# A decoder layer's opening in source order: x in smaller pieces between one-tile weight batches, squares later, idle transposes first

## The chip, the cores and the metric

One core of one Trainium2 chip runs the kernel; the other cores are not used. The metric is the device time of one execution in microseconds, the median of several runs. A difference under 0.2% (some 3.7 us here) can't be told from no change.

## The reference

One layer, batch 1, 256 positions of width 2048, all in fp32. It is a feed-forward half-step, an attention mixture of three head groups, and a second feed-forward half-step:

```python
def swiglu(x, w_gate, w_up, w_down):
    return (jax.nn.silu(x @ w_gate) * (x @ w_up)) @ w_down

x = x + 0.5 * swiglu(rms_norm(x, ffn1_norm[l]), ffn1_gate[l], ffn1_up[l], ffn1_down[l])
h = rms_norm(x, mix_norm[l])
...
x = x + mixed @ w_out[l]
x = x + 0.5 * swiglu(rms_norm(x, ffn2_norm[l]), ffn2_gate[l], ffn2_up[l], ffn2_down[l])
```

The inner width of the feed-forward is 5632. The change concerns only the start of the first gate product, x @ ffn1_gate.

## The kernel before

**Products.** Each fp32 product is made of three fp32r matmuls. A weight is cast to fp32r (`hi`, ACT) and the rest of it is kept as a second fp32r tile (`lo` = raw − hi, DVE). `mm_rows` does, for each of the two 128-row halves of x, hi·wh, hi·wl and lo·wh (L248 to L250), so one 128-row tile of a 512-wide weight block takes six matmuls of 512 columns. Weights come in batches of two such tiles: `load_w` (L198) issues one 512 KB DMA on SP's queue (tile `raw`, four buffers), the ACT cast (L205, three buffers of `hi`) and the DVE subtract (L206, three of `lo`). In the names, `ag` is gate of the first feed-forward, `au` its up weights, and the number is the first tile: `raw_ag_6` holds tiles 6 and 7. `ga` and `ua` are their PSUM accumulators. Gate and up take 16 tiles for each of eleven 512-wide column blocks, always gate, then up.

**x.** The stationary side is x0T, x transposed and scaled by the norm's gain, also as hi and lo. `transpose_chunk` (L213) makes it from 128x128 transposes on PE into a PSUM tile (`tp_x_4` holds tiles 4 to 7; tags `l0` and `l1`, one buffer each), an ACT copy with scale for hi (L226) and a DVE scalar_tensor_tensor for lo, which reads the same PSUM tile and the hi just written (L227). The chunks before are tiles 0-1, 2-3, 4-7, 8-11 and 12-15 (`XCUT`, L109). x is loaded in the same pieces, the first on SP's queue, the others on ACT's.

**Norm.** The row scale (1/rms) is only needed after the first gate block, so the squares of x (`square_sums`, L233 to L236, ACT, eight of 512 columns) run beside the matmuls; `row_rstd` and `rsqrt` then make the scale on DVE.

**Order.** Generators in a class `Lanes` are stepped by `tick` once for each weight batch, and `finish` forces one to its end; `before0` finishes a chunk ahead of the batch that needs it. Beyond the order in which the code emits, the framework's scheduler chooses, for each engine, the order of the instructions by its own priorities. The instructions of an engine then run strictly in that order. `constants` (L139) loads small parameters on POOL's queue, makes masks there, and later transposes the gains (L172, tile `gps`, tag `l0`), copies them to `gT` (L174) and negates the sinks (`nsink`, L178, DVE).

Of the kernel before, what the change touches and what calls it, by code (L numbers as in the profile page):

```python
# [11 lines left out]
AF = mybir.ActivationFunctionType  # L12
ALU = mybir.AluOpType
# [65 lines left out]
def hybrid_layer(ctx, tc, x, mem, ffn1_norm, ffn1_gate, ffn1_up, ffn1_down, mix_norm, mem_norm,  # L79
# [18 lines left out]
    def psum(tag, name):  # L98

        return ps.tile([P, 2, 512], F32, tag=tag, bufs=2 if tag == "acc" else 1, name=name)  # L100

    lanes = Lanes()


    x_sb = cpool.tile([P, NT, D], F32, name="x_sb")
    xv = x.rearrange("(t p) d -> p t d", p=P)
    graw1 = cpool.tile([NK, P], F32, name="graw1")
    nc.scalar.dma_start(graw1, ffn1_norm[0].rearrange("(k p) -> k p", p=P))
    XCUT = ((0, 2), (2, 2), (4, 4), (8, 4), (12, 4))  # L109
    for k0, nk in XCUT:  # L110
        cols = slice(k0 * P, (k0 + nk) * P)
        (nc.scalar if k0 else nc.sync).dma_start(x_sb[:, :, cols], xv[:, :, cols])

    ident = cpool.tile([P, P], F32, name="ident")
    make_identity(nc, ident)
# [2 lines left out]
    warm = cpool.tile([P, 1], F32, name="warm")  # L118
    nc.scalar.activation(warm, ones[:, 0:1], AF.Silu)

    gT = cpool.tile([P, 4 * NK + 6], F32, name="gT")
    gps = psum("l0", "gps1")
    nc.tensor.transpose(gps[:, 0, 0:NK], graw1, ident[0:NK, 0:NK])
    nc.vector.tensor_copy(gT[:, 0:NK], gps[:, 0, 0:NK])
    G_FFN1, G_MIX, G_MEM, G_FFN2, G_HEAD = 0, 16, 32, 48, 64
# [72 lines left out]
    def load_w(w, k0, nk, c0, width, name):  # L198
        raw = wpool.tile([P, KB, 512], F32, tag="raw", bufs=4, name=f"raw_{name}")
        hi = wpool.tile([P, KB, 512], F32R, tag="hi", bufs=3, name=f"hi_{name}")  # L200
        lo = wpool.tile([P, KB, 512], F32R, tag="lo", bufs=3, name=f"lo_{name}")
        r, h, l = (t[:, :nk, :width] for t in (raw, hi, lo))
        nc.sync.dma_start(
            r, w[k0 * P:(k0 + nk) * P, c0:c0 + width].rearrange("(k p) c -> p k c", p=P))
        nc.scalar.copy(h, r)  # L205
        nc.vector.tensor_tensor(out=l, in0=r, in1=h.bitcast(F32), op=ALU.subtract)  # L206
        return h, l
# [2 lines left out]
        nc.scalar.copy(dst_hi, src)  # L210
        nc.vector.tensor_tensor(out=dst_lo, in0=src, in1=dst_hi.bitcast(F32), op=ALU.subtract)

    def transpose_chunk(xT, src, k0, nk, g0, name, pause=1):  # L213

        def stages(tag):
            sv, dst = src(), xT()
            tp = psum(tag, f"tp_{name}")
            tv = tp.rearrange("p a b -> p (a b)").rearrange("p (k s) -> p k s", k=4)
            for k in range(nk):
                for t in range(NT):  # L220
                    nc.tensor.transpose(tv[:, k, t * P:(t + 1) * P], sv[:, t, k * P:(k + 1) * P], ident)
            if pause:
                yield pause
            for k in range(nk):
                g = gT[:, g0 + k0 + k:g0 + k0 + k + 1]
                nc.scalar.activation(dst[:, k0 + k, 0, :], tv[:, k, :], AF.Copy, scale=g)  # L226
                nc.vector.scalar_tensor_tensor(out=dst[:, k0 + k, 1, :], in0=tv[:, k, :], scalar=g,  # L227
                                               in1=dst[:, k0 + k, 0, :].bitcast(F32), op0=ALU.mult,
                                               op1=ALU.subtract)
            yield 1  # L230
        return stages
# [11 lines left out]
    def mm_rows(acc, aT, kt, wh, wl, first, last):  # L243

        w = wh.shape[-1]
        for t in range(NT):
            hi, lo = aT[:, kt, 0, t * P:(t + 1) * P], aT[:, kt, 1, t * P:(t + 1) * P]
            nc.tensor.matmul(acc[:, t, :w], hi, wh, start=first, stop=False)  # L248
            nc.tensor.matmul(acc[:, t, :w], hi, wl, start=False, stop=False)  # L249
            nc.tensor.matmul(acc[:, t, :w], lo, wh, start=False, stop=last)  # L250

    def project(acc, aT, w, c0, width, kts, nk_all, done, name, before=None):

        for k0, n in kts:
            k = k0
            while k < k0 + n:
                b = min(KB, k0 + n - k)
                if before:
                    before(k)
                wh, wl = load_w(w, k, b, c0, width, f"{name}_{k}")  # L260
                for j in range(b):
                    mm_rows(acc, aT, k + j, wh[:, j, :], wl[:, j, :], done == 0, done == nk_all - 1)
                    done += 1
                k += b
                lanes.tick()
        return done


    def ffn(xT, before, stats, wg, wu, wd, after, name):

        with tc.tile_pool(name=f"h_{name}", bufs=1, reuse_waits="tile") as hpool, \
                tc.tile_pool(name=f"ht_{name}", bufs=2, reuse_waits="tile") as htmp:
            hT = hpool.tile([P, NF, 2, SEQ], F32R, name=f"hT_{name}")

            def transpose_h(j, h):

                def stages(tag):
                    tp = psum(tag, f"th_{name}{j}")
# [12 lines left out]
            rstd = None
            for j in range(DFF // 512):
                acc = psum("acc", f"g{name}{j}")
                project(acc, xT, wg, j * 512, 512, [(0, NK)], NK, 0, f"{name}g{j}",
                        None if j else before)
                if j == 0:
                    rstd = stats()
                g = htmp.tile([P, NT, 512], F32, tag="g", bufs=3, name=f"gs{name}{j}")
                for t in range(NT):
                    nc.scalar.activation(g[:, t, :], acc[:, t, :], AF.Silu, scale=rstd[:, t:t + 1])  # L300
                acc = psum("acc", f"u{name}{j}")
                project(acc, xT, wu, j * 512, 512, [(0, NK)], NK, 0, f"{name}u{j}")
                for t in range(NT):
                    nc.vector.scalar_tensor_tensor(out=g[:, t, :], in0=acc[:, t, :],
                                                   scalar=rstd[:, t:t + 1], in1=g[:, t, :],
                                                   op0=ALU.mult, op1=ALU.mult)
                lanes.put(f"hT{name}{j}", transpose_h(j, g))

            def before_d(k):
                if k >= NF - 4:  # L310
                    lanes.finish(f"hT{name}{DFF // 512 - 1}")

            for c in range(4):
                acc = psum("acc", f"d{name}{c}")
# [14 lines left out]
    ss2 = cpool.tile([P, NT, 4], F32, name="ss2")  # L329
    x0T = r1.tile([P, NK, 2, SEQ], F32R, tag="r1", name="x0T")  # L330

    for k0, nk in XCUT:
        cut = x_sb[:, :, k0 * P:(k0 + nk) * P]
        lanes.put(f"aT{k0}", transpose_chunk(lambda: x0T, lambda cut=cut: cut, k0, nk, G_FFN1, f"x0_{k0}", 0))

    def before0(k):
        if k in (0, 2, 4, 8, 12):
            lanes.finish(f"aT{k}")

    def sum_stages(ss, src, c, wait=None):  # L340
        yield 2 + c if wait is None else wait
        square_sums(ss, src(c), c)

    for c in range(4):
        lanes.run(f"ss0_{c}", sum_stages(ss0, xchunk, c))
    lanes.put("consts", constants, ("aT12",))

    memv = mem.rearrange("(t p) d -> p t d", p=P)
    memTs = []
# [22 lines left out]
        square_sums(ss1, xchunk(c), c)  # L372

    def stats0():
        lanes.finish(*(f"ss0_{c}" for c in range(4)))
        return row_rstd(ss0, "x0")

    ffn(x0T, before0, stats0, gate1, up1, down1, after1, "a")
    memT = memTs[0]
    lanes.finish("memT3")  # L380

# [310 lines left out]
        lanes.finish("ss2_3")  # L692
        return row_rstd(ss2, "x2")

    ffn(x2T, lambda k: lanes.finish("bT3") if k == 12 else None, stats2, gate2, up2, down2, store, "b")


# [29 lines left out]
```

## Time and profile before

| | |
|---|---|
| runs of the kernel before | 1846.38 us median of 3 (1846.11 to 1847.82) |
| the profiled execution | 1845.47 us, of which its span is 1843.7 us |
| PE busy | 1829.9 us, 99% of the span |
| PE's share of the chain that ended last | 97% |
| ACT busy, DVE busy | 846.4 us (46%), 938.9 us (51%) |
| HBM read | 339.83 MB, 185 GB/s over the span |

The span is what the hardware profiler recorded of one execution on the core. The first gate matmul starts at 10.23 us of it and the first up matmul at 36.14 us; the change lies in that stretch and the microseconds before it.

### The profile page before, as it was taken

The page shows a single profiled execution, that of the slowest core. Times are in us where ns is not written, and L with a number is a line of the kernel's source. Part 1 is how long each engine was busy: PE and PEld are TensorE (multiplying, and loading weights), DVE is VectorE, ACT ScalarE, POOL GpSimd, SP SyncE. Part 2 cuts the span into 40 slices and gives each one's busy share as a digit, 9 for nine tenths or more (in the row PEclk, how much of TensorE's full clock was granted, in tenths as well). Part 3 has the DMA queues.
Part 4 walks back from the last instruction along what each step waited for, and adds up shares of the span by engine and source line. Part 5 has one row for each costly group of instructions (what it writes and reads, how often), then busy time and mean ns, then how long its engine had stood idle before and what let it go on. Part 6 is the DMA issues. An engine that isn't in the chain of part 4 may idle for free.

```text
span 1843.7 us, 21918 instructions
## 1 busy us (share of the span) xinstructions
PE 1829.9 (99%) x8448; PEld 1538.8 (83%) x8448; DVE 938.9 (51%) x1121; ACT 846.4 (46%) x1148; POOL 11.1 (1%) x31
## 2 busy tenths in 40 slices
PE   8999999999999999999999999999999999999998
PEld 6888888888888888888998888888888888888887
DVE  5554544555445554645655455555555454544443
ACT  6444444444435443656665455444444444433332
POOL 2000000000000000000000000000000000000000
PEclk9999999999999999999999999999999999999999
DMA  7666666666656566565555556666666666666663
GB/s 231 192 189 189 193 186 191 191 188 192 187 191 206 194 210 193 176 175 147 161 143 145 179 181 189 192 186 192 188 190 193 184 192 187 192 194 204 206 204 128
DMA packets 182520, 343.36 MB, mean 186 GB/s; under 512 B 11088, under 2 KB 28048, under 8 KB 182416
## 3 DMA queue, kind: packets, MB, share of 16 engines
q1 hardware_dynamic: 180368, 339.04, 61.6%
q10 hardware_dynamic: 1696, 2.89, 0.4%
q8 instruction: 66, 1.08, 0.3%
q14 instruction: 38, 0.31, 0.1%
q0 software_dynamic: 352, 0.03, 0.0%
HBM read 339.83 MB, written 2.10 MB: 185 GB/s over the span
## 4 chain that ended last, share of the span: by engine, by line
PE 97%; DMA 1%; ACT 1%; DVE 1%; issue 0%; DVEq 0%; ACTq 0%
PE ga L248 4%; PE ga L250 4%; PE ga L249 4%; PE ua L248 4%; PE gb L248 4%; PE db L249 4%; PE db L250 4%; PE gb L249 4%; PE gb L250 4%; PE ub L248 4%; PE ua L249 4%; PE ua L250 4%; PE ub L249 4%; PE ub L250 4%; PE db L248 4%; PE da L249 4%
## 5 line engine op out<-in xcount | busy, mean ns | idle before, releaser
L206 DVE TENSOR_TENSOR lo_bu<-raw_bu,hi_bu 128x1024 fp32r<-128x1024 f32 x88 | 107.8, 1225 | 131.5 <-ACT hi_bu L205 131.5
L206 DVE TENSOR_TENSOR lo_au<-raw_au,hi_au 128x1024 fp32r<-128x1024 f32 x88 | 107.8, 1225 | 130.1 <-ACT hi_au L205 130.1
L206 DVE TENSOR_TENSOR lo_bd<-raw_bd,hi_bd 128x1024 fp32r<-128x1024 f32 x88 | 107.7, 1224 | 124.0 <-ACT hi_bd L205 124.0
L206 DVE TENSOR_TENSOR lo_ad<-raw_ad,hi_ad 128x1024 fp32r<-128x1024 f32 x88 | 107.8, 1224 | 119.5 <-ACT hi_ad L205 119.5
L205 ACT CAST hi_bd<-raw_bd 128x1024 fp32r<-128x1024 f32 x88 | 92.8, 1055 | 145.0 <-PE db L250 139.8
L206 DVE TENSOR_TENSOR lo_ag<-raw_ag,hi_ag 128x1024 fp32r<-128x1024 f32 x88 | 108.1, 1229 | 98.7 <-ACT hi_ag L205 98.7
L206 DVE TENSOR_TENSOR lo_bg<-raw_bg,hi_bg 128x1024 fp32r<-128x1024 f32 x88 | 107.7, 1223 | 99.2 <-ACT hi_bg L205 99.2
L205 ACT CAST hi_ad<-raw_ad 128x1024 fp32r<-128x1024 f32 x88 | 92.7, 1053 | 131.5 <-PE da L250 106.4
L205 ACT CAST hi_bg<-raw_bg 128x1024 fp32r<-128x1024 f32 x88 | 92.7, 1054 | 127.2 <-PE gb L250 68.3
L205 ACT CAST hi_ag<-raw_ag 128x1024 fp32r<-128x1024 f32 x88 | 92.7, 1054 | 122.5 <-PE ga L250 66.3
L205 ACT CAST hi_bu<-raw_bu 128x1024 fp32r<-128x1024 f32 x88 | 92.7, 1054 | 115.5 <-PE ub L250 79.0
L205 ACT CAST hi_au<-raw_au 128x1024 fp32r<-128x1024 f32 x88 | 92.7, 1054 | 115.3 <-PE ua L250 79.4
L248 PE MATMUL ga<-hi_ag,x0T 128*128 128x512 f32 x352 | 138.7, 394 | 0.0
L248 PE MATMUL gb<-hi_bg,x2T 128*128 128x512 f32 x352 | 137.9, 392 | 0.0
L250 PE MATMUL ga<-hi_ag,x0T 128*128 128x512 f32 x352 | 137.3, 390 | 0.0
L249 PE MATMUL ga<-lo_ag,x0T 128*128 128x512 f32 x352 | 137.3, 390 | 0.0
L248 PE MATMUL da<-hi_ad,hT_a 128*128 128x512 f32 x352 | 137.2, 390 | 0.0
L249 PE MATMUL da<-lo_ad,hT_a 128*128 128x512 f32 x352 | 137.1, 389 | 0.1
L250 PE MATMUL gb<-hi_bg,x2T 128*128 128x512 f32 x352 | 137.1, 389 | 0.0
L248 PE MATMUL ua<-hi_au,x0T 128*128 128x512 f32 x352 | 137.0, 389 | 0.0
L248 PE MATMUL db<-hi_bd,hT_b 128*128 128x512 f32 x352 | 137.0, 389 | 0.0
L249 PE MATMUL gb<-lo_bg,x2T 128*128 128x512 f32 x352 | 137.0, 389 | 0.0
(460 smaller groups left out, 3959.7 us busy)
## 6 DMA issues: line engine op xcount, KB each, us to landing
raw_ag<-in_ffn_gate_dram SPq DMA_DIRECT2D x88, 512.0 KB, 4.5
raw_au<-in_ffn_up_dram SPq DMA_DIRECT2D x88, 512.0 KB, 3.7
raw_ad<-in_ffn_down_dram SPq DMA_DIRECT2D x88, 512.0 KB, 4.7
raw_bg<-in_ffn_gate_dram SPq DMA_DIRECT2D x88, 512.0 KB, 4.3
raw_bu<-in_ffn_up_dram SPq DMA_DIRECT2D x88, 512.0 KB, 3.7
raw_bd<-in_ffn_down_dram SPq DMA_DIRECT2D x88, 512.0 KB, 4.6
raw_wo<-in_w_out_dram SPq DMA_DIRECT2D x16, 512.0 KB, 3.7
raw_mk<-in_w_mem_k_dram SPq DMA_DIRECT2D x8, 512.0 KB, 3.8
```

The lines of the kernel that those rows point to most:

```text
L205: nc.scalar.copy(h, r)
L206: nc.vector.tensor_tensor(out=l, in0=r, in1=h.bitcast(F32), op=ALU.subtract)
L248: nc.tensor.matmul(acc[:, t, :w], hi, wh, start=first, stop=False)
L249: nc.tensor.matmul(acc[:, t, :w], hi, wl, start=False, stop=False)
L250: nc.tensor.matmul(acc[:, t, :w], lo, wh, start=False, stop=last)
```

## The change

From the start of the kernel to the end of the first gate block the framework's own ordering is switched off: `opening` is a manual schedule, closed in `stats0`, and each engine gets its instructions in the order of the code there. That order is written anew.

- x is cut into tiles 0, 1, 2-3, 4-5, 6-7, 8-11 and 12-15. The first goes on SP's queue, the next two on ACT's, and the rest on SP's between the weight batches (`XLOAD`).
- The first four weight tiles are batches of one tile (256 KB, a cast and a subtract of 512 columns each); from tile 4 on they are two-tile batches as before. For tile 0 the four matmuls with wh come ahead of the two with wl (`mm_wl_last`).
- The transposes of a chunk, with their evictions, are emitted by `ready0` (`XTRANS`), just after a batch's cast and subtract and ahead of its matmuls: tile 1 at batch 0, tiles 2-3 at 1, 4-5 at 3, 6-7 at 4, 8-11 at 6, 12-15 at 10. The hi of tile 0 is made on DVE (`hi_dve`) in place of ACT.
- The squares of x run after batches 8, 12 and 14 (four in the last place).
- Eight transposes of the identity into a PSUM tile nobody reads (`idle`) stand first on PE. The gains' PSUM tile is moved from tag `l0` to `l1`.

A few column blocks behind the opening the instructions of each engine stand in the same order in both kernels again. Lines move: L205 is L217 after, L206 is L218, L226 is L242 (L239 for `hi_dve`), L227 is L243, L236 is L252, L248 to L250 are L264 to L266, L172 is L184, L174 is L186 and L178 is L190.

ACT around the casts of tiles 6 and 8, before (evictions of chunks `tp_x_4` and `tp_x_8`, squares to `junk`):

```order
L226 ACTIVATE x0T<-tp_x_4_156,gT 128x256
L226 ACTIVATE x0T<-tp_x_8_173,gT 128x256
L205 CAST hi_ag_6_252<-raw_ag_6_251 128x1024
L226 ACTIVATE x0T<-tp_x_4_156,gT 128x256
L226 ACTIVATE x0T<-tp_x_8_173,gT 128x256
L236 ACTIVATE junk,ss_103<-x_sb 128x512 x2
L226 ACTIVATE x0T<-tp_x_4_156,gT 128x256
L226 ACTIVATE x0T<-tp_x_8_173,gT 128x256
L205 CAST hi_ag_8_310<-raw_ag_8_309 128x1024
```

The same place on ACT after the change, from the eviction of tiles 6-7 to the cast of tile 12:

```order
L242 ACTIVATE x0T<-tp_x_6_209,gT 128x256 x2
L217 CAST hi_ag_6_232<-raw_ag_6_231 128x1024
L242 ACTIVATE x0T<-tp_x_8_237,gT 128x256 x4
L217 CAST hi_ag_8_268<-raw_ag_8_267 128x1024
L252 ACTIVATE junk,ss_112<-x_sb 128x512 x2
L217 CAST hi_ag_10_290<-raw_ag_10_289 128x1024
L242 ACTIVATE x0T<-tp_x_12_295,gT 128x256 x4
L217 CAST hi_ag_12_325<-raw_ag_12_324 128x1024
```

Before, the evictions of two chunks are taken in turn, with casts and squares among them. After, all evictions of a chunk follow each other, two or four of them, directly ahead of a cast.

DVE at the end of the gate block, before, with the last chunk's lo and the copy of the gains:

```order
L206 TENSOR_TENSOR lo_ag_14_365<-raw_ag_14_363,hi_ag_14_364 128x1024
L227 SCALAR_TENSOR_TENSOR x0T<-tp_x_12_234,gT,x0T 128x256
L206 TENSOR_TENSOR lo_au_0_407<-raw_au_0_405,hi_au_0_406 128x1024
L227 SCALAR_TENSOR_TENSOR x0T<-tp_x_12_234,gT,x0T 128x256
L206 TENSOR_TENSOR lo_au_2_430<-raw_au_2_428,hi_au_2_429 128x1024
L174 COPY gT<-gps 128x54
L176 TENSOR_SCALAR gT<-gT 128x1 x3
L206 TENSOR_TENSOR lo_au_4_448<-raw_au_4_446,hi_au_4_447 128x1024
```

DVE after the change, from the subtract of tile 3 to that of tile 12:

```order
L218 TENSOR_TENSOR lo_ag_3_183<-raw_ag_3_181,hi_ag_3_182 128x512
L190 TENSOR_SCALAR nsink_107<-sink_106 128x6
L243 SCALAR_TENSOR_TENSOR x0T<-tp_x_4_187,gT,x0T 128x256 x2
L218 TENSOR_TENSOR lo_ag_4_205<-raw_ag_4_203,hi_ag_4_204 128x1024
L243 SCALAR_TENSOR_TENSOR x0T<-tp_x_6_209,gT,x0T 128x256 x2
L218 TENSOR_TENSOR lo_ag_6_233<-raw_ag_6_231,hi_ag_6_232 128x1024
L243 SCALAR_TENSOR_TENSOR x0T<-tp_x_8_237,gT,x0T 128x256 x4
L218 TENSOR_TENSOR lo_ag_8_269<-raw_ag_8_267,hi_ag_8_268 128x1024
L218 TENSOR_TENSOR lo_ag_10_291<-raw_ag_10_289,hi_ag_10_290 128x1024
L243 SCALAR_TENSOR_TENSOR x0T<-tp_x_12_295,gT,x0T 128x256 x4
L186 COPY gT<-gps 128x54
L218 TENSOR_TENSOR lo_ag_12_326<-raw_ag_12_324,hi_ag_12_325 128x1024
```

The subtracts of tiles 6, 8 and 12 now stand behind all of a chunk's lo, the negated sinks stand between the subtract of tile 3 and the lo of tile 4, and the copy of the gains from `gps` has moved from the first up block to a place ahead of the subtract of tile 12. The transposes into `gps` (L184) have moved with it, on PE ahead of the matmuls of tile 12; they take the PSUM buffer `l0` in which `tp_x_12` stood.

```diff
+    opening = ExitStack()
+    opening.enter_context(tc.manual_schedule())
...
-    XCUT = ((0, 2), (2, 2), (4, 4), (8, 4), (12, 4))
-    for k0, nk in XCUT:
+    def load_x(queue, k0, nk):
         cols = slice(k0 * P, (k0 + nk) * P)
-        (nc.scalar if k0 else nc.sync).dma_start(x_sb[:, :, cols], xv[:, :, cols])
+        queue.dma_start(x_sb[:, :, cols], xv[:, :, cols])
+    load_x(nc.sync, 0, 1)
+    load_x(nc.scalar, 1, 1)
+    load_x(nc.scalar, 2, 2)
...
+    idle = psum("l1", "idle")
+    for _ in range(8):
+        nc.tensor.transpose(idle[:, 0, 0:P], ident, ident)
...
-    gps = psum("l0", "gps1")
+    gps = psum("l1", "gps1")
...
             for k in range(nk):
                 g = gT[:, g0 + k0 + k:g0 + k0 + k + 1]
-                nc.scalar.activation(dst[:, k0 + k, 0, :], tv[:, k, :], AF.Copy, scale=g)
+                if hi_dve:
+                    nc.vector.tensor_scalar(out=dst[:, k0 + k, 0, :], in0=tv[:, k, :], scalar1=g,
+                                            scalar2=None, op0=ALU.mult)
+                else:
+                    nc.scalar.activation(dst[:, k0 + k, 0, :], tv[:, k, :], AF.Copy, scale=g)
...
+    def mm_wl_last(acc, aT, kt, wh, wl):
+        for a, w in ((0, wh), (1, wh), (0, wl)):
+            for t in range(NT):
+                nc.tensor.matmul(acc[:, t, :w.shape[-1]], aT[:, kt, a, t * P:(t + 1) * P], w,
+                                 start=a == 0 and w is wh, stop=False)
...
                 wh, wl = load_w(w, k, b, c0, width, f"{name}_{k}")
+                if ready:
+                    ready(k)
                 for j in range(b):
-                    mm_rows(acc, aT, k + j, wh[:, j, :], wl[:, j, :], done == 0, done == nk_all - 1)
+                    if ready and done == 0:
+                        mm_wl_last(acc, aT, k, wh[:, 0, :], wl[:, 0, :])
+                    else:
+                        mm_rows(acc, aT, k + j, wh[:, j, :], wl[:, j, :], done == 0, done == nk_all - 1)
...
+    XLOAD = {3: (4, 2), 4: (6, 2), 6: (8, 4), 8: (12, 4)}
+    XTRANS = {0: (1, 1, "l1"), 1: (2, 2, "l0"), 3: (4, 2, "l1"), 4: (6, 2, "l0"), 6: (8, 4, "l1"),
+              10: (12, 4, "l0")}
...
     def before0(k):
-        if k in (0, 2, 4, 8, 12):
-            lanes.finish(f"aT{k}")
+        if k == 0:
+            transpose_x(0, 1, "l0")
+        if k in XLOAD:
+            load_x(nc.sync, *XLOAD[k])
+
+    def ready0(k):
+        if k in XTRANS:
+            transpose_x(*XTRANS[k])
...
     for c in range(4):
-        lanes.run(f"ss0_{c}", sum_stages(ss0, xchunk, c))
-    lanes.put("consts", constants, ("aT12",))
+        lanes.run(f"ss0_{c}", sum_stages(ss0, xchunk, c, (6, 8, 9, 9)[c]))
+    lanes.run("x0T", after_x0T())
+    lanes.put("consts", constants, ("x0T",))
...
     def stats0():
+        opening.close()
...
-    ffn(x0T, before0, stats0, gate1, up1, down1, after1, "a")
+    ffn(x0T, [(k, 1) for k in range(4)] + [(4, NK - 4)], before0, ready0, stats0, gate1, up1, down1, after1, "a")
```


## Rows read from the trace of the kernel before

**Rows 1.** The page's head: the span, and PE's busy time, share and instructions.

```profile
span 1843.7 us, 21918 instructions
...
PE 1829.9 (99%) x8448; PEld 1538.8 (83%) x8448; DVE 938.9 (51%) x1121; ACT 846.4 (46%) x1148; POOL 11.1 (1%) x31
```

**Rows 2.** Waits of PE: who is waited for, us in total, times, longest us.

```profile
PE tp_x L221 <- DMA x_sb<-in_x_dram: 4.4, 1, 4.4
```

**Rows 3.** PE in order of time: start us, us, what, [idle before <-releaser].

```profile
8.33 1.97 PE L221 MATMUL tp_x<-ident,x_sb 128*128 128x128 f32 x8 [4.42 <-DMA x_sb<-in_x_dram]
...
10.23 0.80 PE L248 MATMUL ga<-hi_ag,x0T 128*128 128x512 f32 x1
...
10.82 0.63 PE L249 MATMUL ga<-lo_ag,x0T 128*128 128x512 f32 x1
...
11.25 0.63 PE L250 MATMUL ga<-hi_ag,x0T 128*128 128x512 f32 x1
...
12.46 0.40 PE L250 MATMUL ga<-hi_ag,x0T 128*128 128x512 f32 x1
```

**Rows 4.** PE in order of time, to the start of the first up block.

```profile
14.07 1.91 PE L221 MATMUL tp_x<-ident,x_sb 128*128 128x128 f32 x16
...
24.04 0.39 PE L250 MATMUL ga<-hi_ag,x0T 128*128 128x512 f32 x1
...
35.63 0.39 PE L250 MATMUL ga<-hi_ag,x0T 128*128 128x512 f32 x1
...
35.95 0.26 PE L172 MATMUL gps<-ident,graw 54*128 54x54 f32 x1
...
36.14 0.50 PE L248 MATMUL ua<-hi_au,x0T 128*128 128x512 f32 x1
```

**Rows 5.** ACT and DVE in order of time, the opening.

```profile
7.75 1.05 ACT L205 CAST hi_ag<-raw_ag 128x1024 fp32r<-128x1024 f32 x1 [2.31 <-DMA raw_ag<-in_ffn_gate_dram]
...
8.83 1.23 DVE L206 TENSOR_TENSOR lo_ag<-raw_ag,hi_ag 128x1024 fp32r<-128x1024 f32 x1 [4.71 <-ACT hi_ag L205]
...
13.31 0.64 ACT L236 ACTIVATE junk<-x_sb 128x512 f32<-128x512 f32 x1
...
15.15 0.47 ACT L226 ACTIVATE x0T<-tp_x,gT 128x256 fp32r<-128x256 f32 x1 [0.16 <-PE tp_x L221]
```

**Rows 6.** DMA issues of the first 30 us: KB each, median us to landing.

```profile
raw_ag<-in_ffn_gate_dram SPq DMA_DIRECT2D x8, 512.0 KB, 6.9
x_sb<-in_x_dram SPq DMA_DIRECT2D x1, 256.0 KB, 3.1
```

**Rows 7.** ACT and DVE in order of time, one chunk of transposes of x2T.

```profile
1090.76 0.47 ACT L226 ACTIVATE x2T<-tp_x,gT 128x256 fp32r<-128x256 f32 x1
...
1092.03 0.48 DVE L227 SCALAR_TENSOR_TENSOR x2T<-tp_x,gT,x2T 128x256 fp32r<-128x256 f32 x1
...
1092.55 0.47 ACT L226 ACTIVATE x2T<-tp_x,gT 128x256 fp32r<-128x256 f32 x1 [1.31 <-DVE x2T L227]
...
1093.05 0.48 DVE L227 SCALAR_TENSOR_TENSOR x2T<-tp_x,gT,x2T 128x256 fp32r<-128x256 f32 x1 [0.54 <-ACT x2T L226]
```

**Rows 8.** ACT in order of time, the opening, two chunks taken in turn.

```profile
17.11 0.84 ACT L226 ACTIVATE x0T<-tp_x,gT 128x256 fp32r<-128x256 f32 x2
17.82 1.06 ACT L205 CAST hi_ag<-raw_ag 128x1024 fp32r<-128x1024 f32 x1
```

**Rows 9.** Groups by line and shape: xcount, busy us, mean ns of one, idle before.

```profile
L210 ACT CAST hT_a<-th_a 128x512 fp32r<-128x512 f32 x22 | 12.8, 582 | 15.5 <-DVE hT_a L211 15.5
...
L211 DVE TENSOR_TENSOR hT_a<-th_a,hT_a 128x512 fp32r<-128x512 f32 x22 | 15.1, 687 | 7.2 <-ACT hT_a L210 7.2
```

**Rows 10.** POOL's load of sink6 and its landing, and DVE's reader of it.

```profile
9.61 0.54 POOL L145 DMA_DIRECT2D sink<-in_swa_sinks_dram  x1
...
sink<-in_swa_sinks_dram POOLq DMA_DIRECT2D x1, 3.0 KB, 5.3
...
17.03 0.16 DVE L178 TENSOR_SCALAR nsink<-sink 128x6 f32<-128x6 f32 x1
```

More of the change, by code (lines that the diff above doesn't have):

```diff
@@ L211, in split, with transpose_chunk @@
         nc.vector.tensor_tensor(out=dst_lo, in0=src, in1=dst_hi.bitcast(F32), op=ALU.subtract)
-    def transpose_chunk(xT, src, k0, nk, g0, name, pause=1):
+    def transpose_chunk(xT, src, k0, nk, g0, name, pause=1, hi_dve=False):
         def stages(tag):
@@ L250, in mm_rows, with project @@
             nc.tensor.matmul(acc[:, t, :w], lo, wh, start=False, stop=last)
-    def project(acc, aT, w, c0, width, kts, nk_all, done, name, before=None):
+    def mm_wl_last(acc, aT, kt, wh, wl):
[3 more added lines that the diff above has]
+                                 start=a == 0 and w is wh, stop=False)
+    def project(acc, aT, w, c0, width, kts, nk_all, done, name, before=None, ready=None):
         for k0, n in kts:
@@ L266, in project, with ffn @@
         return done
-    def ffn(xT, before, stats, wg, wu, wd, after, name):
+    def ffn(xT, starts, before, ready, stats, wg, wu, wd, after, name):
         with tc.tile_pool(name=f"h_{name}", bufs=1, reuse_waits="tile") as hpool, \
@@ L293, in ffn @@
                 acc = psum("acc", f"g{name}{j}")
-                project(acc, xT, wg, j * 512, 512, [(0, NK)], NK, 0, f"{name}g{j}",
-                        None if j else before)
+                if j:
+                    project(acc, xT, wg, j * 512, 512, [(0, NK)], NK, 0, f"{name}g{j}")
+                else:
+                    project(acc, xT, wg, j * 512, 512, starts, NK, 0, f"{name}g{j}", before, ready)
                 if j == 0:
@@ L330, in hybrid_layer, with transpose_x @@
     x0T = r1.tile([P, NK, 2, SEQ], F32R, tag="r1", name="x0T")
-    for k0, nk in XCUT:
+    XLOAD = {3: (4, 2), 4: (6, 2), 6: (8, 4), 8: (12, 4)}
+    XTRANS = {0: (1, 1, "l1"), 1: (2, 2, "l0"), 3: (4, 2, "l1"), 4: (6, 2, "l0"), 6: (8, 4, "l1"),
+              10: (12, 4, "l0")}
+    def transpose_x(k0, nk, tag):
         cut = x_sb[:, :, k0 * P:(k0 + nk) * P]
-        lanes.put(f"aT{k0}", transpose_chunk(lambda: x0T, lambda cut=cut: cut, k0, nk, G_FFN1, f"x0_{k0}", 0))
+        for _ in transpose_chunk(lambda: x0T, lambda: cut, k0, nk, G_FFN1, f"x0_{k0}", 0, k0 == 0)(tag):
+            pass
     def before0(k):
-        if k in (0, 2, 4, 8, 12):
-            lanes.finish(f"aT{k}")
+        if k == 0:
[5 more added lines that the diff above has]
+            transpose_x(*XTRANS[k])
     def sum_stages(ss, src, c, wait=None):
@@ L342, in sum_stages, with after_x0T @@
         square_sums(ss, src(c), c)
+    def after_x0T():
+        yield 9
     for c in range(4):
-        lanes.run(f"ss0_{c}", sum_stages(ss0, xchunk, c))
-    lanes.put("consts", constants, ("aT12",))
+        lanes.run(f"ss0_{c}", sum_stages(ss0, xchunk, c, (6, 8, 9, 9)[c]))
+    lanes.run("x0T", after_x0T())
+    lanes.put("consts", constants, ("x0T",))
     memv = mem.rearrange("(t p) d -> p t d", p=P)
@@ L693, in stats2 @@
         return row_rstd(ss2, "x2")
-    ffn(x2T, lambda k: lanes.finish("bT3") if k == 12 else None, stats2, gate2, up2, down2, store, "b")
+    ffn(x2T, [(0, NK)], lambda k: lanes.finish("bT3") if k == 12 else None, None, stats2, gate2, up2, down2, store, "b")
 _INS = ["x", "mem", "ffn1_norm", "ffn1_gate", "ffn1_up", "ffn1_down", "mix_norm", "mem_norm", "w_in",
```

## The prediction

> **What bounds the kernel now.** The head of the page comes first: PE is busy for 1829.9 of 1843.7 us [rows 1], so away from the ends nothing but PE's own work can be saved, and the change adds none there. What can move is the opening. The waits of PE name one long one, 4.4 us for x [rows 2], and the timeline shows it: PE starts its first eight transposes of x at 8.33, with the landing of tiles 2-3 of x, and the first gate matmul at 10.23 [rows 3]. From there PE hardly stops: matmuls follow each other .43 apart at first (10.82 to 11.25), then, from 12.46 on, .227 apart (51 steps from 24.04 to 35.63), and the first up matmul starts at 36.14 [rows 3, 4]. The gate block has 96 matmuls, so at .227 it takes 21.8 us; with 24 transposes at .109 apart (8.33 to 10.23 holds eight at twice that, 14.07 to 15.74 sixteen) it can't be much denser than it is. The yardstick is therefore the start of the first up matmul: 36.14 before, and what comes after it I take as unchanged.
>
> **What the change gives.** Before, the cast of the first weight batch waits for its landing and starts at 7.75 [rows 5]. The first piece of x on the same queue, 256 KB, lands 3.1 us after its issue [rows 6]. After, a piece of x half as large and a weight tile half as large are first. The weight tile lands between those marks, as an estimate at their middle, 5.4; a cast of half a batch takes .58 [rows 9], and the first gate matmul starts at 6.0. The hi of tile 0 on DVE, .48 like its lo [rows 7], hides behind that landing. The bounds are 5.0 and 8.3, if the small pieces land no sooner than the large ones.
>
> From 6.0 on PE has 21.8 of matmuls, 28 transposes of x at .109 (3.05) and .2 for the gains' transposes (35.95 to 36.14 [rows 4]): 31.05. To this comes the half clock. Spacings of .43 and .22 in place of .227 and .109 show TensorE at the lower of its levels up to 12.46, 2.2 us after the first gate matmul [rows 3]. The six matmuls of tile 0 and the four transposes behind them fall in such a stretch: 6 x .2 + 4 x .11 = 1.6. Without any wait, up would start at 32.7, which is 3.4 us sooner.
>
> **What the change costs.** Waits, and they come from the order on ACT and DVE. Two rows decide them. In one chunk of x2T the second ACT eviction waits 1.31 us for DVE's lo of the tile before, and DVE's next lo waits for that eviction: the lo starts at 1092.03 and 1093.05, so ACT and DVE alternate over one PSUM tile at 1.02 us a tile [rows 7]. Before, the opening hides that, since two chunks are taken in turn: two evictions at 17.11 take .36 each and the cast follows at 17.82 [rows 8]. After, two or four evictions of the same chunk stand together, directly ahead of a cast that PE needs for its next batch.
>
> Let e be the start of a chunk's first eviction. PE has by then worked for .2 on what stands behind the transposes: the eighth of those begun at 14.07 starts at 14.83, PE would go on at 14.94, and the eviction starts at 15.15 [rows 4, 5]. A cast of 1024 takes 1.05 and its subtract 1.23 [rows 5], halves .58 and .69 [rows 9].
>
> - Tile 2, behind two evictions: the second at e+1.02, the cast at e+1.38 to e+1.96, the subtract to e+2.7. PE has six matmuls, so it is ready at e+1.16. It waits .8 for hi, does one matmul, and waits .5 for lo: 1.3.
> - Tiles 4-5, behind two evictions: cast until e+2.44, subtract until e+3.7. PE has six matmuls and four transposes and is ready at e+1.6: .9 and 1.0, together 1.9. Tiles 6-7 then cost nothing: their evictions queue behind that cast, while PE, set back by the wait for lo, still has twelve matmuls and eight transposes (3.6 us).
> - Tiles 8-9, behind four evictions: the last at e+3.06, the cast from e+3.42 to e+4.48, the subtract until e+5.75. PE has twelve matmuls, ready at e+2.5: 2.0 and 1.0, together 3.0.
> - Tiles 12-13: the gains' transposes take the PSUM buffer of that chunk, free only after DVE's fourth lo at about e+4.1. PE is ready at e+2.5 and waits 1.6. It does the transposes, waits .2 for the cast, and 1.0 for the subtract, which stands behind the gains' copy: 2.8.
> - First up batch: four squares of .64 [rows 5] and the row scale's start stand ahead of its cast and subtract, 3.6 us against 2.7 of twelve matmuls, part of which the slack from the last wait covers: .4.
>
> These sum to 9.4. One more wait is new: on DVE the negated sinks stand ahead of the lo of tiles 4-5. Before, POOL issued the sinks' load at 9.61, it took 5.3, and DVE read it at 17.03 without a wait [rows 10]. The place on DVE now comes at about 14.2, the landing at 14.9; the lo, the second eviction, the cast of tiles 4-5 and so PE queue behind it. It costs 0 to .7, I take .3, and each us of a later landing goes straight to PE.
>
> So up starts at 32.7 + 9.4 + .3 = 42.4, which is 6.3 us later than 36.14. The profiled execution took 1845.47 for its span of 1843.7, .9 below the median of the runs, 1846.38. The forecast is 1850.0 for the span, 1851.8 for that execution, and 1852.7 against the median.
>
> At nothing I put: x on SP's queue (weights there take 6.9 us to land [rows 6]; the last piece is issued at about 8 and needed after 25; it would cost only the excess over that); the remaining squares (2 x .64 and a cast against twelve matmuls and a wait for lo); the later Silu (the accumulator has two buffers, and the next gate block starts 21.8 us on); POOL's memset of ones behind the identity.
>
> **The idle transposes.** The eight transposes at 8.33 run .22 apart to the last, and the clock rises only 2.2 us into the matmuls [rows 3]; no row separates whether transposes helped. The Trainium skill, "TensorE: Matmul & The Clock Gate", Part 4 (PE-mode transpose), states that full clock does not engage for transposes, since they don't count as busy in the same way. By that the eight buy nothing and the sum stands; if they count like matmuls, it is the third rival below.
>
> **Rivals.**
> - *Evictions don't alternate with DVE.* If those of a chunk go .36 apart, as at 17.11 [rows 8], casts come sooner: tile 2 costs .6, tiles 4-5 1.2, 8-9 1.0, 12-13 1.3, up .4, together 4.5. Up at 37.2, 1.1 later: 1847.5, no change. Against it stands the named wait [rows 7]; for it, that the row is of another stage. Chance .10.
> - *Faster.* Casts and subtracts keep a batch ahead: a two-tile batch costs ACT 1.05 + 2 x .36 = 1.8 and DVE 1.23 + 2 x .4 = 2.0, PE 3.2. Without waits the time is 1846.4 − 3.4 = 1843.0. It decides when PE's waits up to up sum to less than 3.4. Against it, the cast stands behind all evictions of a chunk, and even at .36 the sum is 4.5. Chance .05.
> - *The idle transposes raise the clock before the first gate matmul.* The 1.6 of half clock goes: 1851.1. Chance .14, since transposes alone didn't raise it before 10.23 [rows 3].
> - *The opening starts no sooner.* The first gate matmul at 8.3, or the half clock holds to about 18 us because PE waits so often: 1.6 to 2.3 more, 1854.3 to 1855.0. Chance .08.
>
> **How the numbers follow.** The main case has .63. The first rival is "same", the second "faster"; all else is over 3.7 us (0.2%, about what a measurement of this kernel tells from no change) above 1846.38: slower .85, same .10, faster .05. The range leaves out the first two rivals (.15) and reaches from under the third, with the sinks at nothing and the landing at 5.0 (1850.3), to the top of the fourth, 1855.0.
>
> **What would show it.** In the changed trace: first gate matmul at 6, first up matmul near 42.4. PE's waits for hi and lo of `ga` sum to about 9, in five places, the largest ahead of tiles 8-9 (3.0) and 12-13 (2.8, with `gps` waiting for DVE). ACT's x0T evictions start 1.0 apart, each with an idle time ended by DVE's x0T. From the third column block on, nothing differs. It is wrong if ACT evictions run .36 apart, if up starts before 38, or if a later block is slower.

## The result and the profile after

The changed kernel is slower: 1858.2 us median of 6 runs (1854.57 to 1860.45) against 1846.61 of 6 (1845.8 to 1847.82); ratio 1.0058, 95% interval 1.0047 to 1.0068, so 11.6 us by the medians and 10.7 by the ratio. The forecast was 1852.7 with a range to 1855.0: the direction is right, the size is nearly twice the forecast, and the time lies outside the range. The execution with the profile took 1857.52.

The head of the page, after:

```profile
span 1855.8 us, 21952 instructions
...
PE 1840.6 (99%) x8456; PEld 1544.5 (83%) x8456; DVE 940.4 (51%) x1124; ACT 847.0 (46%) x1149; POOL 11.4 (1%) x31
```

Against [rows 1], the span is 12.1 us longer and PE's busy time 10.7 longer, with eight matmuls more, the idle transposes, which take 1.97 us. Apart from these PE's work is the same, and waits don't count as busy: matmuls themselves took longer. The waits of PE (us in total, times, longest):

```profile
PE ga L264 <- ACT hi_ag L217: 3.0, 2, 1.8
PE ga L265 <- DVE lo_ag L218: 2.6, 4, 0.8
PE gps L184 <- issue: 1.5, 1, 1.5
```

The two lines on `ga` and the one on `gps` sum to 7.1 (8.9 by the gaps between starts, below); none of the three was there before, when the long wait was for x [rows 2]. The view names no releaser for `gps` ("issue"); it starts at 37.52, and DVE's fourth lo of that chunk runs from 36.93 for .48, so this is the wait for the PSUM buffer that the forecast had. The timeline of PE, in order of time, is the main reading; it is to be held against [rows 3, 4]:

```profile
5.76 2.05 PE L272 MATMUL ga<-hi_ag,x0T 128*128 128x512 f32 x4
...
11.03 0.40 PE L265 MATMUL ga<-lo_ag,x0T 128*128 128x512 f32 x1
...
11.62 0.50 PE L264 MATMUL ga<-hi_ag,x0T 128*128 128x512 f32 x1
...
12.36 0.50 PE L265 MATMUL ga<-lo_ag,x0T 128*128 128x512 f32 x1 [0.23 <-DVE lo_ag L218]
...
15.47 0.60 PE L233 MATMUL tp_x<-ident,x_sb 128*128 128x128 f32 x4
...
17.29 0.49 PE L264 MATMUL ga<-hi_ag,x0T 128*128 128x512 f32 x1 [1.22 <-ACT hi_ag L217]
...
18.55 0.50 PE L265 MATMUL ga<-lo_ag,x0T 128*128 128x512 f32 x1 [0.77 <-DVE lo_ag L218]
...
24.58 0.39 PE L266 MATMUL ga<-hi_ag,x0T 128*128 128x512 f32 x1
...
26.80 0.50 PE L264 MATMUL ga<-hi_ag,x0T 128*128 128x512 f32 x1 [1.83 <-ACT hi_ag L217]
...
28.06 0.78 PE L265 MATMUL ga<-lo_ag,x0T 128*128 128x512 f32 x1 [0.76 <-DVE lo_ag L218]
...
31.58 0.39 PE L264 MATMUL ga<-hi_ag,x0T 128*128 128x512 f32 x1
...
35.67 0.39 PE L266 MATMUL ga<-hi_ag,x0T 128*128 128x512 f32 x1
...
37.52 0.23 PE L184 MATMUL gps<-ident,graw 54*128 54x54 f32 x1 [1.47 <-issue]
...
37.89 0.50 PE L264 MATMUL ga<-hi_ag,x0T 128*128 128x512 f32 x1
...
39.19 0.80 PE L265 MATMUL ga<-lo_ag,x0T 128*128 128x512 f32 x1 [0.80 <-DVE lo_ag L218]
...
45.27 0.40 PE L264 MATMUL ga<-hi_ag,x0T 128*128 128x512 f32 x1
...
47.35 0.39 PE L264 MATMUL ua<-hi_au,x0T 128*128 128x512 f32 x1
```

The first gate matmul starts at 5.76 in place of 10.23, as forecast. The first up matmul starts at 47.35 in place of 36.14, 11.2 later. Three stretches at .43 us a matmul make up most of the difference to the forecast: from 5.76 to 11.03, from 28.06 to 31.58 (eight steps, 3.52 us, where eight at .227 take 1.82), and from 39.19 to 45.27 (fourteen steps, 6.08 where they take 3.18). For the second and the third the windows show the same as the granted clock (third figure from the end; before it the busy times of PE, PEld, DVE, ACT and POOL, behind it DMA share and GB/s):

```profile
26.00:28.00 2.00, 0.50 (x1) 0.19 (x1) 1.55 (x2) 2.00 (x6) 0.00 (x0) 1.00 0.00 0
28.00:30.00 2.00, 1.94 (x5) 1.56 (x6) 1.06 (x2) 0.91 (x1) 0.00 (x0) 0.53 0.42 52
38.00:40.00 2.00, 1.20 (x3) 0.78 (x4) 1.32 (x5) 2.00 (x6) 0.00 (x0) 0.59 0.00 0
```

In the window from 26 PE works for .50 of 2 us and waits; from 28 on the clock is at the lower of its levels, 1.2 in place of 2.4 GHz, for most of the window. The same comes with the waits from 35.9 to 39.2; there the mean of .59 from 38 to 40 means that the clock fell at about 38.4, while PE still waited for lo. For the first stretch the windows read 1.00, as they do for the matmuls of the kernel before that are .43 apart; there the level is read from the spacing alone.

ACT, from the first eviction of tiles 8-11 to the cast of tiles 8-9:

```profile
22.26 0.48 ACT L242 ACTIVATE x0T<-tp_x,gT 128x256 fp32r<-128x256 f32 x1 [1.92 <-PE tp_x L233]
23.29 0.47 ACT L242 ACTIVATE x0T<-tp_x,gT 128x256 fp32r<-128x256 f32 x1 [0.55 <-DVE x0T L243]
...
25.34 0.47 ACT L242 ACTIVATE x0T<-tp_x,gT 128x256 fp32r<-128x256 f32 x1 [0.55 <-DVE x0T L243]
25.71 1.03 ACT L217 CAST hi_ag<-raw_ag 128x1024 fp32r<-128x1024 f32 x1
```

The evictions start 1.03 apart, each held for .55 by DVE's lo of the tile before, as in [rows 7], and the cast comes .37 behind the last. And DVE's reader of the sinks, which waits here, as it did not in [rows 10]:

```profile
15.23 0.17 DVE L190 TENSOR_SCALAR nsink<-sink 128x6 f32<-128x6 f32 x1 [2.33 <-DMA sink<-in_swa_sinks_dram]
```

### The profile page after: what moved, and what is told of

It is laid out like the page before. It is cut to its first block, busy times and chain, and to the rows that moved or that the text cites. A ratio compares the mean times of both kernels' runs of the same rounds, so it can differ in the third digit from the quotient of the medians.

```text
span 1855.8 us, 21952 instructions
## 1 busy us (share of the span) xinstructions
PE 1840.6 (99%) x8456; PEld 1544.5 (83%) x8456; DVE 940.4 (51%) x1124; ACT 847.0 (46%) x1149; POOL 11.4 (1%) x31
## 4 chain that ended last, share of the span: by engine, by line
PE 98%; DMA 1%; DVE 0%; ACT 0%; issue 0%; POOL 0%; DVEq 0%; POOLq 0%; ACTq 0%
PE gb L266 4%; PE da L264 4%; PE db L264 4%; PE gb L264 4%; PE gb L265 4%; PE db L266 4%; PE da L266 4%; PE ub L266 4%; PE ub L265 4%; PE ua L266 4%; PE da L265 4%; PE ua L264 4%; PE ua L265 4%; PE ub L264 4%; PE ga L265 4%; PE db L265 4%
## 5 line engine op out<-in xcount | busy, mean ns | idle before, releaser
L218 DVE TENSOR_TENSOR lo_bu<-raw_bu,hi_bu 128x1024 fp32r<-128x1024 f32 x88 | 107.8, 1225 | 131.5 <-ACT hi_bu L217 131.5
L218 DVE TENSOR_TENSOR lo_au<-raw_au,hi_au 128x1024 fp32r<-128x1024 f32 x88 | 107.8, 1225 | 128.6 <-ACT hi_au L217 128.6
L218 DVE TENSOR_TENSOR lo_bd<-raw_bd,hi_bd 128x1024 fp32r<-128x1024 f32 x88 | 107.8, 1225 | 123.9 <-ACT hi_bd L217 123.9
L218 DVE TENSOR_TENSOR lo_ad<-raw_ad,hi_ad 128x1024 fp32r<-128x1024 f32 x88 | 107.8, 1225 | 119.1 <-ACT hi_ad L217 119.1
L217 ACT CAST hi_bd<-raw_bd 128x1024 fp32r<-128x1024 f32 x88 | 92.8, 1055 | 145.0 <-PE db L266 139.8
L218 DVE TENSOR_TENSOR lo_bg<-raw_bg,hi_bg 128x1024 fp32r<-128x1024 f32 x88 | 107.7, 1224 | 99.1 <-ACT hi_bg L217 99.1
L218 DVE TENSOR_TENSOR lo_ag<-raw_ag,hi_ag 128x1024 fp32r<-128x1024 f32 (+1 forms) x90 | 108.0, 1201 | 95.2 <-ACT hi_ag L217 95.1
L217 ACT CAST hi_ad<-raw_ad 128x1024 fp32r<-128x1024 f32 x88 | 92.7, 1054 | 131.2 <-PE da L266 106.3
L217 ACT CAST hi_bg<-raw_bg 128x1024 fp32r<-128x1024 f32 x88 | 92.7, 1054 | 127.2 <-PE gb L266 68.3
L217 ACT CAST hi_ag<-raw_ag 128x1024 fp32r<-128x1024 f32 (+1 forms) x90 | 92.9, 1033 | 118.7 <-PE ga L266 66.2
L217 ACT CAST hi_bu<-raw_bu 128x1024 fp32r<-128x1024 f32 x88 | 92.7, 1054 | 115.5 <-PE ub L266 79.0
L217 ACT CAST hi_au<-raw_au 128x1024 fp32r<-128x1024 f32 x88 | 92.7, 1054 | 115.3 <-PE ua L266 78.4
L264 PE MATMUL ga<-hi_ag,x0T 128*128 128x512 f32 x350 | 139.8, 400 | 3.2 <-ACT hi_ag L217 3.0
L266 PE MATMUL ga<-hi_ag,x0T 128*128 128x512 f32 x350 | 138.3, 395 | 0.0
L264 PE MATMUL gb<-hi_bg,x2T 128*128 128x512 f32 x352 | 137.9, 392 | 0.0
L264 PE MATMUL da<-hi_ad,hT_a 128*128 128x512 f32 x352 | 137.2, 390 | 0.0
L266 PE MATMUL gb<-hi_bg,x2T 128*128 128x512 f32 x352 | 137.1, 389 | 0.0
L264 PE MATMUL db<-hi_bd,hT_b 128*128 128x512 f32 x352 | 137.0, 389 | 0.0
L266 PE MATMUL da<-hi_ad,hT_a 128*128 128x512 f32 x352 | 137.0, 389 | 0.0
```

## The experiments

The theory is that the whole loss is PE waiting for casts and subtracts that the written order puts too late, and the clock that falls with those waits. The rivals are that the half clock has a cause of its own, that the small pieces or the landings cost, and that the opening needs more of ACT and DVE than PE's work covers. The time of each kernel is the median of its runs; the kernel before ran on the same chip beside it, and the ratio is to that.

**Extra matmuls in the long waits (e2).** Ahead of the matmuls of tiles 8-9 and 12-13, into the PSUM buffer that is free then, 12 and 10 of them:

```diff
+    FILL = {8: ("l0", 12), 12: ("l1", 10)}
...
+            for _ in range(n):
+                nc.tensor.matmul(junk[:, 0, :], x0T[:, 0, 0, 0:P],
+                                 x0T[:, 0, :, :].rearrange("p a s -> p (a s)"), start=True, stop=True)
```

> The changed kernel with extra matmuls into PSUM that nobody reads: 12 ahead of the gate matmuls of tiles 8-9 and 10 ahead of those of tiles 12-13, where PE stood still for 3.0 and 2.9 us; all waits of the kernel's own work stay as they are. Theory 1 (the clock falls because PE stands still there): no stretch at half clock behind tile 8, the first up matmul at 47.35 - 1.5 - 2.9 = 43.0, the time 1858.2 - 4.4 = 1853.8. Theory 2 (the half clock has another cause: the place in the opening, or the load on ACT and DVE): it comes as before, the first up matmul at 47.4, the time 1858.

1853.32, ratio 1.0038 (1.0026 to 1.0051). PE's timeline has the two groups of extra matmuls, behind each the first matmul with lo of that batch, and the first up matmul at 43.31:

```profile
25.20 2.88 PE L388 MATMUL fill<-x0T 128*128 128x512 f32 x12
...
28.45 0.50 PE L265 MATMUL ga<-lo_ag,x0T 128*128 128x512 f32 x1
...
34.70 2.43 PE L388 MATMUL fill<-x0T 128*128 128x512 f32 x10
...
37.96 0.50 PE L265 MATMUL ga<-lo_ag,x0T 128*128 128x512 f32 x1 [0.41 <-DVE lo_ag L218]
...
43.31 0.39 PE L264 MATMUL ua<-hi_au,x0T 128*128 128x512 f32 x1
```

The granted clock is 1.00 in all windows from 14 to 48. From the first lo matmul of tiles 8-9 to that of tiles 12-13 it takes 9.51 us in place of 11.13, and from there to up 5.35 in place of 8.16: 1.6 and 2.8, together 4.4. (Up comes only 4.0 sooner, since x landed later in this execution and the first gate matmul started at 6.68.) More work on PE in the same waits makes the kernel 4.9 us faster by the medians and 3.7 by the ratios, whose intervals just overlap; the timeline is the clearer evidence. So the half clock followed from PE standing still.

**One of the two fills alone (e12, e13), one execution each.**

> The changed kernel with the ten extra matmuls ahead of tiles 12-13 alone, into PSUM that nobody reads. Theory 1 (each stretch at half clock follows its own wait): the stretch of 1.5 us behind tiles 8-9 stays, that of 2.9 behind tiles 12-13 goes, first up matmul near 44.5. Theory 2 (one cause for both, elsewhere): both stay or both go.

> The changed kernel with the twelve extra matmuls ahead of tiles 8-9 alone. Theory 1: the stretch behind tiles 8-9 goes, that behind tiles 12-13 stays, first up matmul near 46. Theory 2: both stay or both go.

These two ran on another chip, on which the kernel before took 1850.54 in its one execution, so their times are not to be set beside 1858.2; the timelines are what they are for. e12 took 1852.3. The fill at 12-13 kept the clock there, but the stretch behind tiles 8-9 did not come either, although PE waited as long as in the changed kernel (1.83 is the wait named for hi), so the first up matmul is at 43.14, not 44.5:

```profile
27.01 0.51 PE L264 MATMUL ga<-hi_ag,x0T 128*128 128x512 f32 x1 [1.83 <-ACT hi_ag L217]
...
28.61 0.40 PE L266 MATMUL ga<-hi_ag,x0T 128*128 128x512 f32 x1
...
34.53 2.43 PE L388 MATMUL fill<-x0T 128*128 128x512 f32 x10
...
43.14 0.39 PE L264 MATMUL ua<-hi_au,x0T 128*128 128x512 f32 x1
```

At 28.61 the matmuls are already .23 apart again (28.61 to 28.84). Taken alone, e12 came out as theory 2 has it: both stretches are gone. But its extra matmuls start at 34.53, long after the wait at tiles 8-9, and can't have kept the clock there; in this execution it did not fall, with nothing done about it. e13 took 1856.29 and came out as theory 1 has it: the fill at 8-9 left the stretch behind 12-13 in place. It ended sooner than in the changed kernel, eight steps on, at 41.16, and the first up matmul starts at 44.59:

```profile
37.63 0.79 PE L265 MATMUL ga<-lo_ag,x0T 128*128 128x512 f32 x1 [0.80 <-DVE lo_ag L218]
```

Over the profiles of the changed kernel, e2, e3, e5, e12 and e13 the count is this. Behind the wait at tiles 8-9 without extra matmuls the clock fell in three of four; behind that at 12-13 in four of four; with extra matmuls in none of four. These waits (for hi, at 12-13 for `gps`, and then for lo, with one matmul between) sum to 2.9 or 3.0 us. At tiles 4-5 they sum to 1.9 to 2.6 in five of the six profiles, and the clock did not fall; in e3 they sum to 2.8, and it fell. So a wait of this size makes the fall possible, and it does not come each time; where in a wait or behind it the fall is decided stays open.

**Without the idle transposes (e3, e10).** The eight transposes of the identity taken out, once of the changed kernel, once of e9 below.

> The changed kernel without the eight idle transposes. Theory 1 (they buy nothing): the clock rises as late as before, near 11, the first gate matmul stays at 5.8 and the time at 1858. Theory 2 (they bring the rise forward): the rise comes later, and every us of half clock more among the first matmuls puts up to 0.5 us on the first up matmul: 1858.5 to 1860.

> e9_cast_first without the eight idle transposes. Theory 1 (they do nothing: the clock rises 2.5 to 5.3 us after the first gate matmul with and without them): time as e9_cast_first, 1843.6, within 1 us. Theory 2 (they bring the rise forward): first up matmul 0.5 to 1.5 later, 1844 to 1845.

e3: 1860.34, ratio 1.0067 (1.0053 to 1.0080); its interval overlaps that of the changed kernel, so no difference can be told.

```profile
8.17 0.60 PE L229 MATMUL tp_x<-ident,x_sb 128*128 128x128 f32 x4
...
17.05 0.51 PE L260 MATMUL ga<-hi_ag,x0T 128*128 128x512 f32 x1 [1.65 <-ACT hi_ag L213]
...
18.31 0.80 PE L261 MATMUL ga<-lo_ag,x0T 128*128 128x512 f32 x1 [0.76 <-DVE lo_ag L214]
```

In its profile the clock had risen by 8.17, where four transposes take .35 to the next matmul at 8.52: that is sooner than with the idle transposes (11.03), against theory 2. It then lost more behind later waits, the first of them at tiles 4-5 (the rows at 17.05 and 18.31), and up started at 48.70. e10: 1844.16, ratio 0.9987 (0.9978 to 0.9996), beside 1843.63 and 0.9981 with them: no difference that can be told. First up matmul 32.87 and 32.73.

**All hi of a chunk, then all lo (e7).** In `transpose_chunk`, for the chunks of x from tile 2 on:

```diff
             for k in range(nk):
                 g = gT[:, g0 + k0 + k:g0 + k0 + k + 1]
+                if hi_first:
+                    nc.scalar.activation(dst[:, k0 + k, 0, :], tv[:, k, :], AF.Copy, scale=g)
+                    continue
...
+            for k in range(nk if hi_first else 0):
+                g = gT[:, g0 + k0 + k:g0 + k0 + k + 1]
                 nc.vector.scalar_tensor_tensor(out=dst[:, k0 + k, 1, :], in0=tv[:, k, :], scalar=g,
                                                in1=dst[:, k0 + k, 0, :].bitcast(F32), op0=ALU.mult,
                                                op1=ALU.subtract)
```

> The changed kernel with the evictions of a chunk of x in another order: all hi on ACT, then all lo on DVE, in place of hi and lo tile by tile. Theory 1 (ACT and DVE alternating over one chunk set the price): hi evictions 0.36 apart in place of 1.02, PE's waits in the gate block from 8.9 down to about 5.5 (ahead of tiles 4-5 2.0, 8-9 1.7, 12-13 1.5), and as none is as long as 3 us the clock stays up: first up matmul near 39, time near 1850. Theory 2 (the casts are late for another reason, such as the landing of the weights): waits as in the changed kernel, time 1857 to 1858.

1849.84, ratio 1.0017 (1.0008 to 1.0026): as theory 1 has it. Longest wait and first up matmul:

```profile
25.00 0.50 PE L273 MATMUL ga<-lo_ag,x0T 128*128 128x512 f32 x1 [1.38 <-DVE lo_ag L218]
...
38.50 0.39 PE L272 MATMUL ua<-hi_au,x0T 128*128 128x512 f32 x1
```

No window between 12 and 48 is below 1.00.

**Evictions behind the next cast (e6).** A chunk is transposed where it was, but evicted by the next batch's `ready0`, behind that batch's cast and subtract; sinks on POOL.

```diff
+        next(gen)
+        if k0 < 2:
+            next(gen)
+        else:
+            pending[k0] = gen
...
     def ready0(k):
+        if k in pending:
+            next(pending.pop(k))
         if k in XTRANS:
             transpose_x(*XTRANS[k])
```

> The changed kernel with a chunk's evictions behind the next weight batch's cast and subtract and the sinks on POOL; hi and lo still tile by tile, so ACT and DVE alternate at 1.02 us a tile. Theory 1 (the place of the cast is what PE waits for): no wait ahead of tiles 2 to 9, but the casts of tiles 10-11 and 14-15 and the first up batch still stand behind four evictions and squares: waits of some 1.6, 1.9 and 0.9, too short for the clock to fall; first up matmul at 37, time near 1848. Theory 2 (only the alternation matters, wherever the cast stands): waits and clock about as in the changed kernel, 1856 or more.

1849.2, ratio 1.0013 (1.0004 to 1.0022). The wait ahead of tiles 8-9 is gone, and the longest is now ahead of tiles 10-11, behind four alternating evictions and two squares (with the wait for lo behind it 2.5 us, and the clock stays up); the first up matmul starts at 37.84:

```profile
26.45 0.50 PE L264 MATMUL ga<-hi_ag,x0T 128*128 128x512 f32 x1 [1.27 <-ACT hi_ag L217]
```

**Sinks on POOL alone (e5), one execution.**

```diff
-        nc.vector.tensor_scalar(out=nsink6, in0=sink6, scalar1=-1.0, scalar2=None, op0=ALU.mult)
+        nc.gpsimd.tensor_scalar(out=nsink6, in0=sink6, scalar1=-1.0, scalar2=None, op0=ALU.mult)
```

> The changed kernel with the negated sinks on POOL in place of DVE, nothing else. Theory 1 (DVE's wait for the sinks' landing at 15.2 goes straight to PE): the wait ahead of tiles 4-5 shrinks from 2.4 to about 1.5 us, the first up matmul comes 0.9 earlier unless the clock falls at other places. Theory 2 (the alternation sets that wait anyway): the wait stays at 2.4.

1856.65, inside the changed kernel's 1854.57 to 1860.45, so its time says nothing. The wait for hi ahead of tiles 4-5 is .71 in place of 1.22, that for lo .76 as before: by the gaps 1.9 in all in place of 2.4, halfway between the two theories. The first up matmul is .9 sooner, but .3 of that is there from the first gate matmul on (5.46 in place of 5.76), since x landed earlier; some .5 is the sinks':

```profile
5.46 2.07 PE L272 MATMUL ga<-hi_ag,x0T 128*128 128x512 f32 x4
...
16.45 0.50 PE L264 MATMUL ga<-hi_ag,x0T 128*128 128x512 f32 x1 [0.71 <-ACT hi_ag L217]
...
46.45 0.39 PE L264 MATMUL ua<-hi_au,x0T 128*128 128x512 f32 x1
```

**The scheduler's order with the new pieces (e4).** The line `opening.enter_context(tc.manual_schedule())` taken out.

> The changed kernel without the manual schedule: the pieces of x, one-tile batches and idle transposes stay, the framework's scheduler orders each engine. Theory 1 (the pieces were good, the written order bad): no wait of 3 us, so no half clock behind the first rise; but the scheduler puts squares and subtracts ahead of the first evictions, so the first gate matmul comes later than 5.8, near 9.7, and the first up matmul near 36: 1846 to 1848. Theory 2 (the pieces themselves cost, by more DMAs on SP's queue or later landings): 1852 or more.

1850.94, ratio 1.0021 (1.0012 to 1.0031): between the two theories. No gate matmul waits over .6 and there is no half clock between 14 and 48, as theory 1 has it, but the transposes of tile 1 wait 5.4 us for DVE's copy of the gains, which the scheduler put behind three subtracts; the first gate matmul starts at 10.44 and the first up matmul at 39.47:

```profile
9.75 0.69 PE L232 MATMUL tp_x<-ident,x_sb 128*128 128x128 f32 x2 [5.42 <-DVE gT L135]
```

So the start that the small pieces make possible is lost again, and more than in the old order; that pieces by themselves cost is not shown here, and e9 speaks against it.

**All three together (e9): hi first, evictions behind the next cast, sinks on POOL.**

> The changed kernel with three edits: hi evictions of a chunk first, then its lo; a chunk's evictions behind the cast and subtract of the next weight batch in place of ahead of them; the negated sinks on POOL in place of DVE. Theory 1 (all that was lost was order on ACT and DVE, and the clock that fell with the waits): PE waits less than 0.5 us in all between the first gate matmul at 5.8 and the first up matmul at 33 to 34, time 1843.5 to 1844.5, below the kernel before. Theory 2 (the opening needs more ACT and DVE time than PE's work covers, whatever the order): waits of over 3.4 us stay, time 1846.6 or more.

1843.63, ratio 0.9981 (0.9973 to 0.9990): 3.5 us faster than the kernel before by the ratio, with the first up matmul 3.4 sooner than there. That is about the .2% that can just be told, but the interval leaves out 1. It keeps the small pieces of x, the one-tile batches, the idle transposes and the hand-written order of the rest, and the casts, subtracts and evictions are the same; so neither the pieces and their landings nor too much work on ACT and DVE can be what the changed kernel lost by. The waits of PE are down to these, none on a hi or lo of `ga`; the last two rows are the first up matmul and ACT's four evictions of tiles 8-11, now .36 apart:

```profile
PE idle L131 <- POOL ident masks.py:199: 1.4, 1, 1.4
...
PE tp_x L233 <- DVE x0T L246: 1.0, 1, 1.0
...
PE sqa L273 <- DVE lo_sqa L218: 0.5, 1, 0.5
...
32.73 0.39 PE L272 MATMUL ua<-hi_au,x0T 128*128 128x512 f32 x1
...
19.12 1.56 ACT L239 ACTIVATE x0T<-tp_x,gT 128x256 fp32r<-128x256 f32 x4
```

## Why the forecast was right in sign and wrong in size

- **The start.** 6.0 was forecast, 5.76 measured: the landing at the middle of its bounds was a good estimate.
- **The waits at each batch.** Forecast, then measured from the rows after (the gap between starts less .227 for the matmul ahead): tile 2 1.3 and .6; tiles 4-5 with the sinks 2.2 and 2.4 (the sinks .3 and, by e5, some .5); tiles 8-9 3.0 and 2.0 + 1.03; tiles 12-13 2.8 and 1.6 + .2 + 1.07; first up batch .4 and 0. The sum is 9.7 and 8.9. At tile 2 and at the up batch the half clock that ran then covered part of the wait (in e12, without it, 1.1 and .15). The mechanism, ACT and DVE alternating at 1.02 us a tile ahead of the cast, is shown by ACT's rows, by e7 (order inside a chunk alone, up 8.9 sooner) and by e6 (place of the cast, up 9.5 sooner, some .5 of it the sinks').
- **The step that failed is the half clock.** The text said: "The six matmuls of tile 0 and the four transposes behind them fall in such a stretch: 6 x .2 + 4 x .11 = 1.6." It gave the half clock to the start alone. Measured, the first stretch lasts until 11.03, 5.3 us behind the first gate matmul in place of 2.2, and holds six matmuls, four transposes and four matmuls more: 5.27 us for work of 2.7, so 2.6 in place of 1.6. And two further stretches came behind the two long waits, 1.6 and 2.8 us by the comparison with e2, which the sum did not have at all. By the forecast up would start at 42.4; −.2 for the start, −.8 for the waits, +1.0 and +4.4 for the half clock give 46.8, and .6 are left for handovers between transposes, waits and matmuls (as 12.36 to the next at 12.69, .33 in place of .23). With PE kept at work in the same waits, in e2, the 4.4 are gone, and up starts at 43.3, .9 from the forecast.
- **The rival that named it was priced at the wrong place.** Its words, "the half clock holds to about 18 us because PE waits so often", shared a chance of .08 and reached 1855.0 at most; how its price follows from rows is not said. The mechanism was near, but the clock rose at 11.03 and fell again later. A wait of 3 us was priced at 3 us; the two long ones cost 4.6 and 5.7.
- **The other rivals.** Evictions of one chunk, taken by themselves, ran .36 apart only where the code emits all its hi first (e9). The idle transposes did not bring the clock up: it rose 5.3 us behind the first gate matmul with them in the changed kernel, 2.5 in e9 with them, 2.6 in e3 and 3.6 in e10 without them. This agrees with what the Trainium skill, "TensorE: Matmul & The Clock Gate", Part 4 (PE-mode transpose), states, that transposes don't count as busy in the same way as matmuls, without proving it. Once the clock was up, transposes ran at full clock too: the four at 13.63 took .35 us to the next matmul, those at 8.47, ahead of the rise, .71.
- **What comes behind the opening.** I took it as unchanged. From the first up matmul to the end the span still lost .9. Some 1.4 are lost in the mixture, in a half-clock stretch that both kernels have (the same ACT cast starts at 981.63 and 992.36 ahead of it, 10.7 apart, the same ACT square at 998.75 and 1010.90 near its end, 12.2 apart); .5 had been regained before it. Windows of the kernel before, then of the changed one:

```profile
992.00:996.00 4.00, 4.00 (x10) 2.25 (x10) 0.95 (x3) 1.86 (x8) 0.00 (x0) 0.50 0.01 4
996.00:1000.00 4.00, 4.00 (x16) 3.82 (x17) 2.97 (x10) 0.50 (x2) 0.00 (x0) 0.65 0.00 0
```

```profile
1000.00:1004.00 4.00, 4.00 (x11) 2.08 (x10) 2.31 (x6) 0.59 (x3) 0.00 (x0) 0.61 0.34 98
1004.00:1008.00 4.00, 4.00 (x10) 2.11 (x9) 0.00 (x0) 1.27 (x6) 0.00 (x0) 0.50 0.00 0
1008.00:1012.00 4.00, 4.00 (x14) 3.82 (x15) 2.82 (x9) 0.49 (x2) 0.00 (x0) 0.61 0.00 0
```

The instructions there are the same; before, the stretch is seen in two windows of 4 us, after in three. Why its length differs is not shown.

## What to carry to other kernels

An order written by hand is to be checked at each place where two engines read one tile in turn: emit all of the first engine's work, then all of the second's, and put work that the bottleneck needs next (here the cast) ahead of work that it needs later. A wait of the bottleneck engine can cost more than its length, since TensorE may work at half clock for some us behind it (here 3.5 and 6.1); price both. And a gain at the start (here 4.5 us) is only kept if the batches behind it keep that pace, so the sum is made up to the first point where nothing waits any more.

## What the runs showed of the hardware that was not expected

- With waits of about 3 us PE's matmuls ran at the lower clock for 3.5 and 6.1 us in the changed kernel; behind the same wait at tiles 8-9 in e12 the clock did not fall.
- Work that nobody reads made a kernel faster: 22 extra matmuls, 5.0 us of PE time, took it from 1858.2 to 1853.3 (ratios 1.0058 and 1.0038).
- The first rise of the clock, read from the spacing, came 2.5 to 5.3 us behind the first gate matmul in kernels with the same first microseconds (e9 and the changed kernel).
